# A quarter of layer B's input projection in seven block products instead of eight

## The chip, the cores and the metric

The kernel runs on one core of a Trainium2 chip. The core has a matrix engine (TensorE, PE in the profile), a vector engine (VectorE, DVE), a scalar engine (ScalarE, ACT), a general engine (GpSimd, POOL) and a queue that issues the transfers (SyncE, SP). Each engine works through its own list of instructions in order, and semaphores between the engines tell when an operand is ready or a buffer is free. Matmuls read their operands from SBUF and write to PSUM, which has eight banks of 128 x 512 float32 values.

The metric is the device time of one execution in microseconds. "Before" is the median of three runs.

## The reference

The reference is a two-layer encoder trunk for 256 tokens of width 2048 in float32. Layer A uses latent attention with 16 heads, layer B differential attention with 8 heads. Both add their result to the residual. What matters here is layer B:

```
z = rms_norm(x, norm_g) @ w_in            # 2048 -> 8192
q, k, v, gate = split(z)                  # 2048 each, 8 heads of 256
q, k = rms_norm per half head (128), times gains
p = softmax(q1 k1 + bias) - lam * softmax(q2 k2 + bias)
o = rms_norm(p @ v, subln) * (1 - lam_init)
out = x + (o * silu(gate)) @ w_out        # 2048 -> 2048
```

The projection `x @ w_in` is 256 x 2048 times 2048 x 8192.

## The kernel before

**Precision by splitting.** [...] To come near float32, each operand is split into a high part (a cast) and a low part (the value less the high part), and each product is made of three matmuls, `mm3`: high x high, low x high, high x low (lines 122 to 125). The three appear in the profile as L123, L124 and L125.

**Weights.** The weights stream from memory in chunks of 256 rows (two contraction tiles of 128) by 512 columns. `stream` (line 105) loads a chunk into one of four `raw` buffers (SP), ACT casts it into `whi` (L118), and DVE subtracts to give `wlo` (L119). There are three `whi` and three `wlo` buffers, so splits run at most some two chunks ahead of PE. `project` (line 127) then does 12 matmuls of width 512 a chunk: two contraction tiles, two token tiles of 128, three parts.

**Tokens.** The activations stand feature-major: `x1h` and `x1l` hold, for each of 16 contraction tiles, 128 features by 256 tokens. They are the stationary operand, the weights move.

**Layer B by heads.** For head h, block 2h of the weights gives q and k (512 columns), accumulated in the two PSUM banks of pool `psg` (named pg), and block 2h+1 gives v and the gate, in pool `psu` (pu). Each block is 8 chunks. Around them stand, per head:

- `qk_b`: squares of q and k by ACT (junk), a sum on DVE (ssb), a reciprocal root on POOL (fb), a multiplication on DVE (qk)
- `qk_t`: transposes of qk by PE (ptb), split by ACT and DVE into bh and bl
- `soft_b`: scores (psb), softmax and difference (eb) on DVE and ACT
- `p_b`: transposes of eb (ptpb), split into phb and plb
- `vg_b`: v split into vhb and vlb, the gate (sgb)
- `av_b`: the product with v (pob, 12 matmuls of width 256), then the sub-norm: ACT squares (junk), DVE (sso), POOL's root (fo), DVE (fo), and the gated result gob
- `go_b`: transposes of gob (pto), split into goh2 and gol2 for the output projection

The functions are called in an order that puts several chunks of the projections between one step and the next (lines 744 to 758), so that PE has matmuls to do while the other engines work through a chain. The final order on each engine is set when the program is scheduled: instructions that are ready in the scheduler's own reckoning can move ahead of others on their engine.

Between the layers, `add_a` adds layer A's output to the residual, and `x1_t(n)` transposes a quarter of it (ptx) and splits it into x1h and x1l. The last, `x1_t(3)`, follows the first two chunks of head 0's q and k.

## Time and profile before

| quantity | value |
|---|---|
| runs | 847.14, 847.34, 848.98 us; median 847.34 |
| span of the profiled execution (first to last instruction) | 845.0 us |
| median of the runs less that span | 2.3 us |
| busy PE, DVE, ACT, POOL in the span | 835.9, 564.6, 488.0, 86.4 us |
| one head of layer B (from ptb to ptb) | 48.29 us |
| granted TensorE clock, mean | 1.000 |

Rows of the timeline start with the start time and the length, both in us from the span's start; then come the engine, the line, the operation, and what is written from what; "x2" means that several instructions were merged into one row, whose length runs from the first's start to the last's end. In square brackets stands how long the engine was idle before, and what it waited for. A matmul's length counts its way through the array, so matmuls in a row overlap: their starts give the pace. Rows of the windows give a stretch, its length, busy time and number of instructions of PE, PE's weight loads, DVE, ACT and POOL, then the granted clock, the busy share of the DMA engines and GB/s. Grouped rows give the total busy time, the mean in ns, and the idle time before.

### The profile page before, as it was taken

How to read it: one execution, taken by the hardware profiler on the slowest of the kernel's cores; microseconds unless marked ns; L12 is line 12 of the kernel's file. 1: busy time of each engine (PE TensorE's matmuls, PEld its weight loads, DVE VectorE, ACT ScalarE, POOL GpSimd, SP SyncE). 2: the span in 40 equal slices, each digit the busy share in tenths (PEclk: the TensorE clock that was granted, in tenths of full speed). 3: DMA queues.
4: the chain of work that ended last, by engine and by line, in shares of the span. 5: the costliest groups of instructions: out<-in, count | busy, mean ns of one | idle time of the engine just before them, and what ended most of it. 6: DMA issues, size and time to landing. Idle time of an engine off the chain costs nothing.

```text
span 845.0 us, 11706 instructions
## 1 busy us (share of the span) xinstructions
PE 835.9 (99%) x4187; PEld 714.5 (85%) x4187; DVE 564.6 (67%) x968; ACT 488.0 (58%) x995; POOL 86.4 (10%) x113
## 2 busy tenths in 40 slices
PE   8999999999999999999999999999999999999998
PEld 6988888889888888888888888888888888888886
DVE  6968678788787866555647565565756566565543
ACT  7656687677767656555555465555555564554331
POOL 2300221122202200000010010010001000000000
PEclk9999999999999999999999999999999999999999
DMA  8755544534444645555555555554555555455661
GB/s 268 256 197 162 166 147 146 176 116 162 144 144 149 248 154 180 180 186 177 185 175 174 175 175 175 175 175 150 193 181 175 175 175 171 168 184 198 219 211 70
DMA packets 42954, 148.59 MB, mean 176 GB/s; under 512 B 5008, under 2 KB 6032, under 8 KB 42640
## 3 DMA queue, kind: packets, MB, share of 16 engines
q1 hardware_dynamic: 42896, 147.84, 52.5%
q8 instruction: 33, 0.54, 0.3%
q14 instruction: 25, 0.20, 0.1%
HBM read 145.73 MB, written 2.10 MB: 175 GB/s over the span
## 4 chain that ended last, share of the span: by engine, by line
PE 94%; DVE 3%; DMA 1%; ACT 1%; issue 0%; SPq 0%; POOL 0%; DVEq 0%; ACTq 0%
PE pu L123 14%; PE pu L125 14%; PE pu L124 14%; PE pg L124 13%; PE pg L123 13%; PE pg L125 13%; DVE wlo L119 1%; PE ptb L651 1%; PE ptn L430 1%; PE ptp L484 1%; PE pa L124 1%; DMA raw<-in_wz 1%; PE pa L125 1%; PE pa L123 1%; DVE xl L152 1%; PE ps L462 0%
## 5 line engine op out<-in xcount | busy, mean ns | idle before, releaser
L119 DVE TENSOR_TENSOR wlo<-raw,whi 128x1024 fp32r<-128x1024 f32 (+4 forms) x278 | 328.6, 1191 | 189.8 <-ACT whi L118 189.5
L118 ACT CAST whi<-raw 128x1024 fp32r<-128x1024 f32 (+3 forms) x277 | 282.2, 1025 | 233.6 <-PE pg L125 102.6
L123 PE MATMUL pu<-whi,x1h 128*128 128x512 f32 x256 | 101.3, 396 | 0.0
L123 PE MATMUL pg<-whi,x1h 128*128 128x512 f32 x256 | 100.5, 392 | 0.0
L125 PE MATMUL pu<-whi,x1l 128*128 128x512 f32 x256 | 99.9, 390 | 0.0
L124 PE MATMUL pu<-wlo,x1h 128*128 128x512 f32 x256 | 99.8, 390 | 0.0
L124 PE MATMUL pg<-wlo,x1h 128*128 128x512 f32 x256 | 99.7, 390 | 0.0
L125 PE MATMUL pg<-whi,x1l 128*128 128x512 f32 x256 | 99.7, 389 | 0.0
L125 PEld LDWEIGHTS pu<-whi,x1l 128*128 128x128 f32 x256 | 48.1, 188 | 10.2
L125 PEld LDWEIGHTS pg<-whi,x1l 128*128 128x128 f32 x256 | 48.1, 188 | 10.1
L123 PEld LDWEIGHTS pg<-whi,x1h 128*128 128x128 f32 x256 | 48.1, 188 | 9.5
L124 PEld LDWEIGHTS pg<-wlo,x1h 128*128 128x128 f32 x256 | 48.1, 188 | 9.4
L124 PEld LDWEIGHTS pu<-wlo,x1h 128*128 128x128 f32 x256 | 48.2, 188 | 9.2
L123 PEld LDWEIGHTS pu<-whi,x1h 128*128 128x128 f32 x256 | 48.1, 188 | 9.2
L123 PE MATMUL pg<-whi,xh 128*128 128x512 f32 (+1 forms) x128 | 49.8, 391 | 1.9 <-ACT whi L118 1.3
L124 PE MATMUL pg<-wlo,xh 128*128 128x512 f32 (+1 forms) x128 | 48.7, 381 | 1.9 <-DVE wlo L119 1.9
L123 PE MATMUL pg<-whi,goh 128*128 128x512 f32 x128 | 50.5, 395 | 0.0
L123 PE MATMUL pu<-whi,goh 128*128 128x512 f32 x128 | 50.1, 392 | 0.0
L124 PE MATMUL pg<-wlo,goh 128*128 128x512 f32 x128 | 49.9, 390 | 0.0
L125 PE MATMUL pg<-whi,gol 128*128 128x512 f32 x128 | 49.9, 390 | 0.0
L124 PE MATMUL pu<-wlo,goh 128*128 128x512 f32 x128 | 49.9, 390 | 0.0
L125 PE MATMUL pu<-whi,gol 128*128 128x512 f32 x128 | 49.9, 389 | 0.0
(246 smaller groups left out, 1551.1 us busy)
## 6 DMA issues: line engine op xcount, KB each, us to landing
raw<-in_wB SPq DMA_DIRECT2D x128, 512.0 KB, 3.2
raw<-in_wgA SPq DMA_DIRECT2D x32, 512.0 KB, 3.5
raw<-in_woA SPq DMA_DIRECT2D x32, 512.0 KB, 3.3
raw<-in_woB SPq DMA_DIRECT2D x32, 512.0 KB, 3.2
raw<-in_wkvu SPq DMA_DIRECT2D x16, 512.0 KB, 4.3
raw<-in_wz SPq DMA_DIRECT2D x15, 544.0 KB, 5.7
raw<-in_wqu SPq DMA_DIRECT2D x16, 384.0 KB, 3.1
x<-in_x SPq DMA_DIRECT2D x1, 2048.0 KB, 10.0
```

Source lines behind the costliest of these rows:

```text
L118: (V.tensor_copy if after_first and a == 0 else A.copy)(hi[:, a:b], raw[:, a:b])
L119: V.tensor_tensor(lo[:, a:b], raw[:, a:b], f32(hi[:, a:b]), ALU.subtract)
L123: T.matmul(o, shi, mhi, start=start, stop=False)
L124: T.matmul(o, shi, mlo, start=False, stop=False)
L125: T.matmul(o, slo, mhi, start=False, stop=stop)
L152: V.scalar_tensor_tensor(lo, src, g, f32(hi), ALU.mult, ALU.subtract)
L430: T.transpose(pt[:, h, t * P:(t + 1) * P], src[:, t, h, :NOPE], ident)
L484: T.transpose(pt[:, c, t * P:(t + 1) * P], e[:, t, c * P:(c + 1) * P], ident)
L651: T.transpose(pt[:, m, t * P:(t + 1) * P], qk[:, t, 2 * i + m, :], ident)
```

## The change

The first two of the eight chunks of each block (`FAST = 2`, a quarter of the contraction) are no longer multiplied straight. They are taken as a 2 x 2 by 2 x 2 block product: rows are the two token tiles, the inner index is the first or second contraction tile of a chunk, columns are the head's two weight blocks (q and k, v and gate). Straight that is eight block products, each summed over the two chunks. The change forms seven, by a known scheme:

- On the token side four sums of x tiles, made once after `x1_t(0)` by `sums`: ACT scales, POOL adds and subtracts, ACT and DVE split them into `sh` and `sl`.
- On the weight side four differences per head, t1, t2, t3 and t4, by DVE from the row blocks b11, b12, b21 and b22. `rows` loads a row block with one transfer (the same contraction tile of both chunks, 512 columns each). b22 is loaded twice.
- `form` splits a difference or a row block in the buffers whi and wlo (named fhi and flo), and `product` does 6 matmuls of width 512 with it, for two chunks and three parts.
- Four products (`shared`, steps 0 to 3) go to a PSUM bank of the pool `patt` (named pa), and ACT and DVE join them in SBUF in the tiles d0 to d3. The other three start the accumulation of the remaining six chunks in pg (two of them) and pu (one).
- `qk_b` and `vg_b` first add the accumulated banks into d0 and d2, or d1 and d3, and go on from these SBUF tiles where they read PSUM before.

The `shared` steps of head h+1 are called between the chunks of v and gate of head h; for head 0 all of them come in a row after layer A, with the first two products of its q and k, ahead of `x1_t(3)`. To make room in SBUF, buffers that only layer A uses go into a pool `la` that is closed ahead of layer B's pool `lb`.

Two places show how the order moves. The first is PE at head 2's `av_b` and `go_b`, where buffer numbers tell the tiles apart (fhi_5419 and flo_5420 hold the split of t4, whi_5430 the next chunk). Before, the transposes and their neighbours:

```order
L124 MATMUL pg_5211<-wlo_5311,x1h_3548 128x512
L125 MATMUL pg_5211<-whi_5310,x1l_3549 128x512
L733 MATMUL pto_5327<-ident_81,gob_5270 128x128 x4
L123 MATMUL pg_5210<-whi_5337,x1h_3548 128x512
L124 MATMUL pg_5210<-wlo_5338,x1h_3548 128x512
```

In the change:

```order
L128 MATMUL pob_5447<-vlb_5380,phb_5350 128x256
L129 MATMUL pob_5447<-vhb_5379,plb_5351 128x256
L839 MATMUL pto_5526<-ident_84,gob_5469 128x128 x2
L127 MATMUL pg_5404<-fhi_5419,x1h_3557 128x512
L839 MATMUL pto_5526<-ident_84,gob_5469 128x128 x2
L127 MATMUL pg_5403<-whi_5430,x1h_3557 128x512
L128 MATMUL pg_5404<-flo_5420,x1h_3557 128x512
```

Before, three chunks (36 matmuls) of the next head's q and k stood between pob and pto; now the transposes of gob follow pob's last matmul directly, and the product with t4 comes behind the first two of them. The second place is DVE at the same point of the program. Before, from the gate to gob:

```order
L669 SCALAR_TENSOR_TENSOR sgb_5201<-sgb_5201,pu_4991 128x256
L119 TENSOR_TENSOR wlo_5293<-raw_5291,whi_5292 128x1024
L119 TENSOR_TENSOR wlo_5311<-raw_5309,whi_5310 128x1024
L719 TENSOR_SCALAR sso_5261<-sso_5261 128x2
L722 TENSOR_TENSOR fo_5267<-fo_5267,r1h_4020 128x2
L725 SCALAR_TENSOR_TENSOR gob_5270<-pob_5248,fo_5267,sgb_5201 128x256 x2
```

In the change, from the second join of vg_b (L766; the first stands just ahead) to the split of t4:

```order
L766 TENSOR_TENSOR d3_4790<-pu_5141,d3_4790 128x512
L156 SCALAR_TENSOR_TENSOR vlb_5380<-d1_4788,r1x_4100,vhb_5379 128x256
L775 SCALAR_TENSOR_TENSOR sgb_5381<-sgb_5381,d1_4788 128x256
L676 TENSOR_TENSOR d1_5239<-pa_5390,d1_5239 128x512
L156 SCALAR_TENSOR_TENSOR vlb_5380<-d3_4790,r1x_4100,vhb_5379 128x256
L775 SCALAR_TENSOR_TENSOR sgb_5381<-sgb_5381,d3_4790 128x256
L677 TENSOR_TENSOR d3_5241<-pa_5390,d2_5240 128x512
L690 TENSOR_TENSOR t1_5417<-rows_5405,t2_5233 128x1024
L825 TENSOR_SCALAR sso_5460<-sso_5460 128x2
L828 TENSOR_TENSOR fo_5466<-fo_5466,r1h_4102 128x2
L831 SCALAR_TENSOR_TENSOR gob_5469<-pob_5447,fo_5466,sgb_5381 128x256 x2
L160 TENSOR_TENSOR flo_5420<-t1_5417,fhi_5419 128x1024
```

Joins and the difference t4 (in t1's buffer) now stand between the gate and the sub-norm, and the split of t4 behind gob.

The core of the diff, with renamed buffers of layer A left out:

```diff
+FAST = 2
...
+    only_a.close()
+    lb = ctx.enter_context(tc.tile_pool(name="lb", bufs=1))
...
+    def sums(c, pt):
+        xf = lb.tile([P, 2, S], F32, tag="t1", name="xf", padded_shape=[P, 2, 512])
+        for j in range(2):
+            A.activation(xf[:, j, :], pt[:, j, :], AF.Copy, scale=gB_t[:, 2 * c + j:2 * c + j + 1])
+        x00, x01, x10, x11 = (xf[:, j, t * P:(t + 1) * P] for t in range(2) for j in range(2))
+        s = lb.tile([P, 4, P], F32, tag="t3", name="s", padded_shape=[P, 8, P])
+        G.tensor_tensor(s[:, 0], x10, x11, ALU.add)
+        G.tensor_tensor(s[:, 2], x00, x10, ALU.subtract)
+        G.tensor_tensor(s[:, 1], s[:, 0], x00, ALU.subtract)
+        G.tensor_tensor(s[:, 3], x01, s[:, 1], ALU.subtract)
+        split(sh[:, c], sl_[:, c], s)
...
+    def form(src):
+        hi = wp.tile([P, 1024], F32R, tag="whi", name="fhi", padded_shape=[P, WCH])
+        lo = wp.tile([P, 1024], F32R, tag="wlo", name="flo", padded_shape=[P, WCH])
+        split(hi, lo, src)
+        return hi, lo
...
+    def product(o, lhs, src, start, stop):
+        hi, lo = form(src)
+        for c in range(FAST):
+            sl = slice(c * 512, (c + 1) * 512)
+            mm3(o, *lhs(c), hi[:, sl], lo[:, sl], start and c == 0, stop and c == FAST - 1)
...
+    def shared(h, i):
+        if i == 0:
+            b11, b12, b22 = rows(2 * h, 0), rows(2 * h + 1, 0), rows(2 * h + 1, 1)
+            t1, t2, t3 = t_tile("t1"), t_tile("t2"), t_tile("t3")
+            V.tensor_tensor(t1, b12, b11, ALU.subtract)
+            V.tensor_tensor(t3, b22, b12, ALU.subtract)
+            V.tensor_tensor(t2, b22, t1, ALU.subtract)
+            state["t", h] = (b11, t2, t3, t1)
+            state["d", h] = [lb.tile([P, 512], F32, tag=f"d{j}", name=f"d{j}", bufs=1 + j % 2) for j in range(4)]
+        d11, d12, d21, d22 = state["d", h]
+        p = bank(patt)
+        product(p, (own(0, 0), summed(1), summed(2), summed(0))[i], state["t", h][i], True, True)
+        if i == 0:
+            A.copy(d11, p)
+        elif i == 1:
+            V.tensor_tensor(d12, p, d11, ALU.add)
+        elif i == 2:
+            V.tensor_tensor(d21, p, d12, ALU.add)
+        else:
+            V.tensor_tensor(d12, p, d12, ALU.add)
+            V.tensor_tensor(d22, p, d21, ALU.add)
...
+    def qk_mm(h, n):
+        if n == 0:
+            state["qa", h] = pair(psg)
+        acc = state["qa", h]
+        if n < 2:
+            b21 = state["b21", h] = rows(2 * h, 1) if n == 0 else state["b21", h]
+            if n == 0:
+                product(acc[0], own(0, 1), b21, True, False)
+            else:
+                t4 = t_tile("t1")
+                V.tensor_tensor(t4, b21, state["t", h][1], ALU.subtract)
+                product(acc[1], own(1, 1), t4, True, False)
+        else:
+            rest(acc, 2 * h, n - 2 + FAST, False)
+
+    def vg_mm(h, n):
+        if n == 0:
+            state["va", h] = pair(psu)
+            product(state["va", h][0], summed(3), rows(2 * h + 1, 1), True, False)
+        else:
+            rest(state["va", h], 2 * h + 1, n - 1 + FAST, n == 1)
...
-    mm_b(0, psg, 0, 2)
+    for i in range(4):
+        shared(0, i)
+    for n in range(2):
+        qk_mm(0, n)
     x1_t(3)
...
+    def qk_b(h):
+        d = state["d", h][0::2]
+        for t, acc in enumerate(state.pop(("qa", h))):
+            V.tensor_tensor(d[t], acc, d[t], ALU.add)
...
+    def vg_b(h):
+        d = state.pop(("d", h))[1::2]
+        for t, acc in enumerate(state.pop(("va", h))):
+            V.tensor_tensor(d[t], acc, d[t], ALU.add)
...
+    NQ, NV = 2 + KC - FAST, 1 + KC - FAST
...
     for h in range(BH):
-        vg_b(h, 0, 3)
+        last = h + 1 == BH
+        vg_steps(h, 0, 3)
         qk_t(h)
-        vg_b(h, 3, 5)
+        vg_steps(h, 3, 4)
+        if not last:
+            shared(h + 1, 0)
+        vg_steps(h, 4, 5)
         soft_b(h)
-        vg_b(h, 5, 7)
+        if not last:
+            shared(h + 1, 1)
+        vg_steps(h, 5, 6)
+        if not last:
+            shared(h + 1, 2)
         p_b(h)
-        vg_b(h, 7, KC)
...
+        vg_steps(h, 6, NV)
...
+            shared(h + 1, 3)
+            qk_steps(h + 1, 0, 3)
+            av_b(h)
+            qk_steps(h + 1, 3, 6)
+            go_b(h)
+            qk_steps(h + 1, 6, NQ)
```

## The prediction

> **What bounds the kernel now.** I read the page's busy times first, then its chain of work that ended last, then the windows over the heads of layer B.

> ```profile
> PE 835.9 (99%) x4187; PEld 714.5 (85%) x4187; DVE 564.6 (67%) x968; ACT 488.0 (58%) x995; POOL 86.4 (10%) x113
> ...
> PE 94%; DVE 3%; DMA 1%; ACT 1%; issue 0%; SPq 0%; POOL 0%; DVEq 0%; ACTq 0%
> ```

> TensorE is the bound and fills 94% of the chain. One head of layer B, between one ptb transpose and the next, in the windows (length, then busy time of each engine):

> ```profile
> 445.97:494.26 48.29, 48.29 (x234) 40.54 (x233) 29.87 (x48) 26.54 (x53) 3.79 (x3) 1.00 0.52 175
> ```

> PE never idles in 48.29 us; VectorE has 18.4 us spare, ScalarE 21.8. So taking matmuls away pays in full, as long as those two keep far enough ahead of PE. The price of a matmul comes from the first and last of 35 consecutive ones in the timeline (start, length):

> ```profile
> 429.70 0.39 PE L124 MATMUL pg<-wlo,x1h 128*128 128x512 f32 x1
> ...
> 437.42 0.39 PE L125 MATMUL pg<-whi,x1l 128*128 128x512 f32 x1
> ```

> 34 steps in 7.72 us: 0.227 us each, so a weight chunk of 12 matmuls holds PE for 2.72 us and a product of 6 for 1.36. The vector prices, back to back, are two chunk subtractions and two 512-wide adds of PSUM into SBUF; beside them one ScalarE cast:

> ```profile
> 492.67 2.35 DVE L119 TENSOR_TENSOR wlo<-raw,whi 128x1024 fp32r<-128x1024 f32 x2
> 366.41 1.28 DVE L568 TENSOR_TENSOR x<-pu,x 128x512 f32<-128x512 f32 x2
> 491.57 1.05 ACT L118 CAST whi<-raw 128x1024 fp32r<-128x1024 f32 x1 [1.19 <-PE pu L125]
> ```

> A single subtraction lasts 1.22,

> ```profile
> L119 DVE TENSOR_TENSOR wlo<-raw,whi 128x1024 fp32r<-128x1024 f32 x240 | 292.0, 1224 | 177.6 <-ACT whi L118 177.6
> ```

> so in the pair the first makes way after 1.13; a 512-wide add costs 0.64.

> **What is removed.** The two fast chunks cost 48 matmuls a head and will cost 7 x 2 x 3 = 42. Over 8 heads 48 matmuls go: 48 x 0.227 = **10.9 us** less PE work, and a head's own PE work falls to 48.29 - 1.36 = 46.93.

> **What is added off PE.** Per head three more splits and four weight differences (t1 to t4), 7 x 1.13 = 7.9 us of DVE, and eight 512-wide joins, 8 x 0.64 = 5.1: DVE goes from 29.87 to about 42.9 of 46.93. ACT gets three casts and a copy, some 3.8 us, and stands near 30. Both fit as totals, so the sum by totals alone costs them at nothing. But DVE keeps only 4 us of slack, and its work comes in bunches where PE has only 1.36 us per split. Loads become 17 instead of 16 of 512 KB a head; DMA was 0.52 busy in the window above, and all raw buffers come round a chunk or more before they are needed, so I price them at nothing and keep a late load as a rival.

> **What is moved: the transposes of go.** This is the largest term. Before, 36 matmuls stood between the last pob matmul and the pto transposes, from 469.12 to 477.31 below. In the changed order the pto transposes stand directly behind pob, in heads 0 to 6. What lies between the two is the chain of the sub-norm:

> ```profile
> 469.00 0.28 PE L125 MATMUL pob<-vhb,plb 128*128 128x256 f32 x1
> 469.12 0.40 PE L123 MATMUL pg<-whi,x1h 128*128 128x512 f32 x1
> 469.32 0.39 ACT L718 ACTIVATE junk<-pob 128x256 f32<-128x256 f32 x1 [0.34 <-PE pob L125]
> 470.34 0.17 DVE L719 TENSOR_SCALAR sso<-sso 128x2 f32<-128x2 f32 x1
> 470.59 0.69 POOL L92 TENSOR_TENSOR fo<-sso,nhalf 128x2 f32<-128x2 f32 x1 [14.42 <-DVE sso L719]
> 471.32 0.16 DVE L722 TENSOR_TENSOR fo<-fo,r1h 128x2 f32<-128x2 f32 x1 [0.81 <-POOL fo L92]
> 471.51 0.88 DVE L725 SCALAR_TENSOR_TENSOR gob<-pob,fo,sgb 128x256 f32<-128x256 f32 x2
> ...
> 477.31 0.60 PE L733 MATMUL pto<-ident,gob 128*128 128x128 f32 x4
> ```

> PE is free of pob at 469.12, and the first gob tile is there at 471.51 + 0.44 = 471.95. With a tenth for the signal PE must wait 2.9 us at pto. Two waits stand beside it:
> - Ahead of pob. The value tiles vhb and vlb now need the joins of d1 and d3 first. After pu's last matmul DVE has about 0.5 of a split left, then two joins 1.28, vlb 0.40, sgb 0.36, a third join 0.64 and the second vlb 0.40, together 3.6. PE has two products (2.72) and the three pob matmuls (0.36) that need only the first tile. It waits about 0.6.
> - Behind pto. The split of t4 stands after gob on DVE and takes 1.13 from the end of the second gob (0.44 after the first); PE has the four transposes and two matmuls meanwhile, about 0.9. It waits about 0.7.

> The vlb and sgb steps are these rows:

> ```profile
> 462.96 0.48 DVE L152 SCALAR_TENSOR_TENSOR vlb<-pu,r1x,vhb 128x256 fp32r<-128x256 f32 x1 [0.20 <-ACT vhb L151]
> 463.36 0.41 DVE L669 SCALAR_TENSOR_TENSOR sgb<-sgb,pu 128x256 f32<-128x256 f32 x1
> ```

> Sum 0.6 + 2.9 + 0.7 = 4.2 us a head, seven times: **+29.4**. Behind the waiting transposes on PE stand t4's product and all chunks of the next q and k; nothing else there can run. Bounds: 0, 2.8 and 0.3 if DVE comes early (3.1 a head; no wait can be below nothing, and the chain has nothing left to drop); 1.5, 3.5 and 1.5 if it comes a split late (6.5). I take the middle, from the rows.

> **The ptb transposes, all heads.** From pg's end to q and k normalised took

> ```profile
> 485.45 0.28 ACT L637 ACTIVATE junk<-pg 128x128 f32<-128x128 f32 x1 [0.95 <-PE pg L125]
> ...
> 485.93 0.39 PE L123 MATMUL pu<-whi,x1h 128*128 128x512 f32 x1
> ...
> 491.46 1.29 DVE L641 TENSOR_TENSOR qk<-pg,fb 128x512 f32<-128x512 f32 x2 [1.75 <-POOL fb L92]
> ...
> 494.10 1.03 PE L651 MATMUL ptb<-ident,qk 128*128 128x128 f32 x8
> ```

> PE left pg at 485.93, so the first qk tile was ready 6.2 later (491.46 + 0.64) and PE came at 8.2. Now a join stands first (+0.7), ACT casts one chunk ahead of the squares and one more among them (+0.85, +1.05), and a split stands ahead of the second ssb (+0.4): ready at 9.2, while PE comes after a product, two chunks and seven matmuls, 1.36 + 5.44 + 1.59 = 8.39. That is a wait of 0.8 in seven heads, 0.4 in the last, which has no next head to prepare: **+6.0**; bounds 0 and 12.

> **The start.** Six products follow out_a(3) in a row. From its end until the first whole chunk's low half is there, DVE does two adds (1.28), four splits and t4 (5 x 1.13), four joins (2.56), four x1l (2 x 0.87), small ones (0.7) and that low half (1.13), in all 13.1, with about 0.8 of waiting for casts: 13.9. PE then has 11 matmuls left (2.5) and is through at 16.4, where its own work is 6 x 1.36 + 0.87 (the ptx transposes) + 2.72 = 11.75. **+4.6**; bounds 2.5 and 6.5.

> ```profile
> 374.57 0.87 DVE L152 SCALAR_TENSOR_TENSOR x1l<-ptx,gains_t,x1h 128x256 fp32r<-128x256 f32 x2
> ...
> 372.31 0.87 PE ptx L576 x8
> ```

> **The token sums.** Two chains of four 128x128 operations on POOL, priced by

> ```profile
> L413 POOL TENSOR_TENSOR rt<-qn,ropc 128x128 f32<-128x128 f32 x16 | 11.6, 728 | 52.2 <-ACT qn L403 52.2
> ```

> at 2.9 us each. ACT waits for them in its queue, ahead of two weight casts whose cover was 2.72 us: **+1.5**, bounds 0 and 3.

> **Sum.** -10.9 + 29.4 + 6.0 + 4.6 + 1.5 = +30.6. The profiled execution's span is 845.0 and the median of the runs 847.34, so 2.3 lies around it: 875.6 + 2.3 = **878 us**. The bounds together: -10.9 + 21.7 + 0 + 2.5 + 0 = +13 (861), and -10.9 + 45.5 + 12 + 6.5 + 3 = +56 (903), which needs every term at its worst.

> **Rivals.**
> 1. Short waits. Only what the order forces is paid: 3.35 a head at pto, 0.2 at ptb, 3 at the start: -10.9 + 23.5 + 1.6 + 3 = +17, **864.5**. For it: DVE has slack elsewhere and idled on casts in every chunk of the trace. Against: these places are where its added work is bunched. 0.16.
> 2. The clock drops in the new waits. At the trace's end PE is idle after 840.87 + 0.24:

> ```profile
> 840.87 0.24 PE pu L125
> 844.40:844.70 0.30, 0.00 (x0) 0.00 (x0) 0.00 (x0) 0.00 (x0) 0.00 (x0) 0.85 0.00 0
> 844.70:845.00 0.30, 0.00 (x0) 0.00 (x0) 0.00 (x0) 0.00 (x0) 0.00 (x0) 0.50 0.00 0
> ```

> The granted clock (the number before the last two) goes from 1.00 to 0.50 some 3.5 us after the last matmul. My wait is 2.9 with hardly a microsecond of work in the 1.6 after it. If it trips the gate, each head runs some 3.4 us at half speed and loses 1.7: 7 x 1.7 = 12 more, **890**. 0.14. [...]
> 3. A load is late. Four raw buffers now hold up to three row blocks at once, in pieces half as long. If a load lands in twice the page's 3.2 us in the bunch of each head, 2.5 more per head: 7 x 2.5 = 17, **895**. 0.05.

> ```profile
> raw<-in_wB SPq DMA_DIRECT2D x128, 512.0 KB, 3.2
> ```

> 4. Not slower: the wait at pto is covered. If PE's waits per head come below (10.9 - 4.6 - 1.5) / 7 = 0.7 us, the saving decides; with none the time is 847.3 - 10.9 + 6.1 = **842.5**. It needs the sub-norm chain in a quarter of the 2.9 us that its rows show, or other matmuls between pob and pto, and the order has none. 0.03. That the matmuls are not taken away is no rival: the changed order has 1,488 of them in this projection for 1,536.

> **How the numbers follow.** The first forecast has 0.62 (its own range 866 to 889). Rivals 1 to 4 have 0.16, 0.14, 0.05 and 0.03. Eight in ten lie between the short waits, opened a little below, and the dropped clock: 862 to 892. A measurement tells 0.2%, 1.7 us, from no change. Faster: rival 4 less a part, 0.02; same 0.01; slower 0.97.

> **What would show it.** In the changed trace: PE idle of 2.5 to 3.5 us before pto with gob as its releaser, seven times; idle before pob put to vlb, and before t4's product to its split; PE about 836 - 11 busy; DVE about 43 us in a head of 51 to 53; ptb waiting for qk by under 1.5; some 4 us of PE idle after out_a(3); granted clock 1.00 throughout. It is wrong if PE shows no gap between pob and pto, or if the largest idle is put to DMA.

## The result, and the profile after

The changed kernel takes 896.11 us (891.53 to 899.48) where the kernel before takes 847.59 beside it: a ratio of 1.0569, 95% interval 1.0541 to 1.0596. It is slower, as forecast, but by 48.5 us and not by 31, and it lies outside the range of 862 to 892.

The page of the changed kernel, busy times and the shares of its chain:

```profile
PE 852.6 (95%) x4139; PEld 719.3 (80%) x4139; DVE 664.4 (74%) x1090; ACT 517.6 (58%) x1033; POOL 98.2 (11%) x121
...
PE 80%; DVE 7%; ACT 5%; POOL 3%; issue 2%; DMA 2%; SPq 0%; DVEq 0%; ACTq 0%
```

TensorE has 48 matmuls fewer and is busy 16.7 us longer (835.9 before). So its instructions ran longer. The view by core gives the span and the mean granted clock:

```profile
core 0: 897.7 us, clock 0.976
```

It was 1.000 before: 2.4% of 897.7, some 21 us, is lost to half clock. What TensorE waited for in the changed kernel (us in total, times, longest):

```profile
PE pto L839 <- DVE gob L831: 19.6, 7, 2.8
PE ptb L756 <- DVE qk L746: 12.6, 8, 1.9
PE pg L128 <- DVE flo L160: 2.2, 5, 0.8
PE pg L127 <- ACT fhi L159: 1.9, 1, 1.9
```

The seven waits at pto, 2.8 us each with gob as their releaser, are the ones of the forecast. Windows of 2 us around the first of them (length, then busy time of PE, PEld, DVE, ACT and POOL with counts; the third number from the end is the granted clock):

```profile
429.00:431.00 2.00, 0.82 (x7) 0.62 (x6) 1.75 (x3) 1.11 (x5) 0.00 (x0) 1.00 0.00 0
431.00:433.00 2.00, 0.40 (x3) 0.41 (x3) 1.15 (x5) 2.00 (x3) 0.70 (x1) 0.71 0.65 186
433.00:435.00 2.00, 2.00 (x8) 1.66 (x7) 2.00 (x2) 1.14 (x2) 0.00 (x0) 0.50 0.19 76
435.00:437.00 2.00, 2.00 (x6) 1.52 (x6) 1.73 (x3) 0.26 (x1) 0.00 (x0) 0.50 0.39 102
437.00:439.00 2.00, 2.00 (x7) 1.56 (x6) 1.19 (x2) 1.16 (x2) 0.00 (x0) 0.58 0.80 291
439.00:441.00 2.00, 2.00 (x11) 1.61 (x10) 0.43 (x2) 0.70 (x1) 0.00 (x0) 1.00 0.59 205
```

Once PE is back at work it fits 6 to 8 matmuls into 2 us and not 11, until the clock returns. The same stands behind every pto in half-microsecond windows: the clock is at 0.50 for 3.41 us, sometimes for 6.83, and 1.7 or 3.4 us are lost. It stands behind the start too (377 to 384.5) and behind one ptb (681). Together these stretches lose 20.5 us; another 0.8 us lies behind the last matmul. In the stretch of layer B, changed kernel and then before:

```profile
360.00:842.00 482.00, 445.58 (x2006) 363.91 (x2005) 360.50 (x524) 258.55 (x480) 35.40 (x24) 0.96 0.52 167
```

```profile
360.00:842.00 482.00, 481.09 (x2279) 402.50 (x2277) 287.65 (x428) 248.86 (x464) 28.21 (x23) 1.00 0.53 176
```

PE's idle time went from 0.9 to 36.4 us. The spans differ by 52.7: 35.5 of idle time, 20.5 of half clock, less 10.9 of matmuls, and 7.6 that are recorded as busy. An estimate gives 4.5 of these: in each of the seven heads pob's fifth and sixth matmul together start 0.3 us late, and ahead of each of the fifteen waits at pto and ptb the last matmul counts some 0.16 us more than its pace, while it goes through the array (0.28 us for 0.12, or 0.39 for 0.227). The rest is open. DVE fills a head as forecast:

```profile
408.70:464.05 55.35, 50.77 (x227) 41.52 (x227) 42.13 (x63) 29.95 (x57) 4.76 (x3) 0.94 0.50 162
```

42.1 us of it (42.9 forecast), ACT 29.95 (30), while the head has grown to 53 to 57 us.

### The profile page after: what moved, and what is told of

It is laid out like the page before. It is cut to its first block, busy times and chain, and to the rows that moved or that the text cites. A ratio compares the mean times of both kernels' runs of the same rounds, so it can differ in the third digit from the quotient of the medians.

```text
span 897.7 us, 11799 instructions
## 1 busy us (share of the span) xinstructions
PE 852.6 (95%) x4139; PEld 719.3 (80%) x4139; DVE 664.4 (74%) x1090; ACT 517.6 (58%) x1033; POOL 98.2 (11%) x121
## 4 chain that ended last, share of the span: by engine, by line
PE 80%; DVE 7%; ACT 5%; POOL 3%; issue 2%; DMA 2%; SPq 0%; DVEq 0%; ACTq 0%
PE pg L128 12%; PE pg L129 12%; PE pg L127 12%; PE pu L129 9%; PE pu L128 9%; PE pu L127 9%; PE pa L128 2%; PE pa L129 2%; PE pa L127 2%; POOL fb L96 2%; DVE flo L160 2%; ACT whi L122 2%; ACT junk L742 1%; DVE wlo L123 1%; PE ptb L756 1%
## 5 line engine op out<-in xcount | busy, mean ns | idle before, releaser
L123 DVE TENSOR_TENSOR wlo<-raw,whi 128x1024 fp32r<-128x1024 f32 (+3 forms) x246 | 289.3, 1187 | 143.2 <-ACT whi L122 142.6
L122 ACT CAST whi<-raw 128x1024 fp32r<-128x1024 f32 (+4 forms) x245 | 247.7, 1021 | 193.1 <-PE pg L129 99.4
L129 PE MATMUL pg<-whi,x1l 128*128 128x512 f32 x192 | 77.5, 404 | 0.0
L127 PE MATMUL pu<-whi,x1h 128*128 128x512 f32 x192 | 76.7, 400 | 0.0
L128 PE MATMUL pu<-wlo,x1h 128*128 128x512 f32 x192 | 76.1, 396 | 0.0
L129 PE MATMUL pu<-whi,x1l 128*128 128x512 f32 x192 | 75.3, 392 | 0.0
L129 PE MATMUL pg<-whi,xl 128*128 128x512 f32 (+1 forms) x128 | 48.7, 381 | 0.0
L159 ACT CAST fhi<-t 128x1024 fp32r<-128x1024 f32 x32 | 33.5, 1046 | 23.8 <-PE pu L129 20.4
L129 PE MATMUL pu<-whi,m 128*128 128x384 f32 (+1 forms) x128 | 46.4, 362 | 0.0
L127 PE MATMUL pu<-whi,m 128*128 128x384 f32 (+1 forms) x128 | 46.4, 362 | 0.0
L128 PE MATMUL pu<-wlo,m 128*128 128x384 f32 (+1 forms) x128 | 46.3, 362 | 0.0
## 6 DMA issues: line engine op xcount, KB each, us to landing
raw<-in_wB SPq DMA_DIRECT2D x96, 512.0 KB, 4.0
rows<-in_wB SPq DMA_DIRECT2D x40, 512.0 KB, 4.2
raw<-in_wgA SPq DMA_DIRECT2D x32, 512.0 KB, 3.4
raw<-in_woA SPq DMA_DIRECT2D x32, 512.0 KB, 3.5
raw<-in_woB SPq DMA_DIRECT2D x32, 512.0 KB, 3.2
raw<-in_wkvu SPq DMA_DIRECT2D x16, 512.0 KB, 4.1
```

What stands on the lines that cost most here:

```text
L122: (V.tensor_copy if after_first and a == 0 else A.copy)(hi[:, a:b], raw[:, a:b])
L123: V.tensor_tensor(lo[:, a:b], raw[:, a:b], f32(hi[:, a:b]), ALU.subtract)
L127: T.matmul(o, shi, mhi, start=start, stop=False)
L128: T.matmul(o, shi, mlo, start=False, stop=False)
L129: T.matmul(o, slo, mhi, start=False, stop=stop)
L159: A.copy(hi, src)
```

## The experiments

Two theories were at hand. **The clock**: the waits come out nearly as forecast, and a wait of 2.8 us is enough to halve the clock behind it. **VectorE's load**: 42 us of vector work in a head stall TensorE wherever they stand, and the low clock only follows from that. A third reading, waits alone with a clock that drops for another reason, was kept beside them.

**1. The moved transposes alone, in the kernel before.** All eight block products; only TensorE's order is forced.

```diff
-        av_b(h)
-        nxt(2, 5)
-        go_b(h)
-        nxt(5, KC if h + 1 < BH else 7)
+        if h + 1 < BH:
+            with tc.issue_after(state["mm"].ins):
+                av_b(h)
+            go_b(h)
+            with tc.issue_after(state["pto"].ins):
+                nxt(2, KC)
...
```

`state["mm"]` is the last matmul of the two chunks ahead, `state["pto"]` the last transpose.

> The kernel before, with all eight block products, in which only the order on TensorE is forced: in heads 0 to 6 the four pto transposes stand directly behind the twelve pob matmuls and all further chunks of the next head's q and k behind pto. Nothing else is changed. Theory of the clock: a wait of 2.8 us at pto is enough to halve the granted clock behind it, so each head pays 2.8 and some 2.2 of half clock: 847.5 + 7 x 5.0 = 882 us (875 to 890), with a granted clock of 0.50 within 3 us behind every pto. Theory of the waits alone (the low clock of the changed kernel has another cause, such as its products of six matmuls): 847.5 + 7 x 2.8 = 867 us (864 to 870), granted clock 1.00. Theory of VectorE's load (the wait is long because VectorE has 42 us of work in a head): with VectorE at 30 us a head the wait is under 2 us and the time under 862.

Measured: 880.14 us, ratio 1.0389 (1.0373 to 1.0404). What TensorE waited for at pto:

```profile
PE pto L733 <- DVE gob L725: 19.6, 7, 2.8
```

Four windows around the second pto, with columns as above:

```profile
474.00:476.00 2.00, 0.50 (x5) 0.29 (x3) 1.40 (x2) 1.15 (x5) 0.20 (x1) 1.00 0.61 225
476.00:478.00 2.00, 0.73 (x4) 0.63 (x5) 1.04 (x3) 0.00 (x0) 0.50 (x1) 0.61 0.75 242
478.00:480.00 2.00, 2.00 (x7) 1.61 (x6) 0.52 (x2) 0.95 (x2) 0.00 (x0) 0.50 0.06 25
480.00:482.00 2.00, 2.00 (x6) 1.55 (x5) 0.44 (x1) 0.00 (x0) 0.00 (x0) 0.50 0.00 0
```

VectorE is busy for 3.4 of these 8 us, and the wait is the same 2.8 us and the clock falls the same way: seven waits make 19.6 us, and the half clock in this trace loses 13.7. The theory of the clock said 882, the waits alone 867, VectorE's load under 862. So the place of these four transposes alone, with none of the seven-product change in it, costs 33 us, two thirds of the 48.

**2. Work in the wait.** The changed kernel with 24 matmuls more in each of heads 0 to 6.

```diff
+        if h + 1 < BH:
+            hot = patt.tile([P, NT, BV], F32, tag="pa", name="hot")
+            for _ in range(2):
+                for t in range(NT):
+                    tq = slice(t * P, (t + 1) * P)
+                    for c in range(2):
+                        mm3(hot[:, t, :], ph[:, c, tq], pl[:, c, tq], vh[:, c, :], vl[:, c, :], c == 0, c == 1)
```

> The changed kernel with 24 matmuls more in each of heads 0 to 6: the pob products twice over into a bank that nobody reads, between pob and pto, so that TensorE has some 2.9 us of work where it waits 2.8. The outputs stay those of the reference. Theory of the clock: the low clock that now costs some 15 of 20.5 us behind pto goes, and the time falls although work is added: 896 - 15 + 7 x 0.5 = 884 us (880 to 889). Theory of the waits alone: nothing is gained and a little lost, 896 + 7 x 0.6 = 900 us (897 to 903).

Measured: 884.18 us, ratio 1.0441 (1.0425 to 1.0456): 11.9 us less than the changed kernel, with 168 matmuls added. Its span and clock, and what TensorE waited for:

```profile
core 0: 882.6 us, clock 0.998
```

```profile
PE ptb L756 <- DVE qk L746: 10.7, 8, 1.8
...
PE pto L846 <- DVE gob L838: 1.7, 7, 0.2
```

The chain that pto waits for is no shorter here (the first gob is written 2.7 to 2.8 us after pob's end in both kernels, and pto starts 4.9 to 5.0 us after pob's first matmul, for 4.6 to 4.7); only the idle time is filled. That the time falls all the same shows that the low clock behind pto cost at least these 11.9 us.

**3. t4's product late.** Three whole chunks can run between pob and pto.

```diff
-            qk_mm(h, n)
+            qk_mm(h, (0, 2, 3, 4, 1, 5, 6, 7)[n] if h > 0 else n)
```

> The changed kernel, in which for heads 1 to 7 the product with t4 is taken behind three whole chunks of q and k and not ahead of them, so that those chunks can run between pob and pto; t4 itself is still formed early. Same matmuls, same VectorE work. Theory of the pto wait with the clock: what stands between pob and the next v and g now costs 39 us more than its matmuls; without the wait 896 - 39 = 857 us (853 to 863), no idle time put to gob, no low clock behind pob. Theory of the waits alone: 896 - 20 = 876 us (873 to 879). Theory of VectorE's load: the stall comes back at the next place where TensorE needs a split, and the time stays over 885.

Measured: 867.56 us, ratio 1.0246 (1.0225 to 1.0266): 28.5 us less, where the clock said 39 and the waits alone 20. What TensorE waits for now:

```profile
PE ptb L762 <- DVE qk L752: 14.3, 8, 1.9
PE pg L128 <- DVE wlo L123: 7.8, 10, 1.2
```

No wait at pto is left, and the mean granted clock is 0.997, with one drop. But a new wait stands behind pob, 0.8 us in each head: the low half of the next chunk, whose subtraction is queued on VectorE behind the joins and the v and g steps. This is the part of the load theory that holds: a stall taken away comes back smaller at the next place.

**4. GpSimd's power beside a subtraction, in the kernel before.** In the changed kernel the power for fb takes 2.5 us where it took 1.64, and a subtraction runs with it. Head 1 of the changed kernel:

```profile
460.46 1.22 DVE L662 TENSOR_TENSOR t<-rows 128x1024 f32<-128x1024 f32 x1
...
460.63 2.54 POOL L96 TENSOR_TENSOR fb<-ssb,nhalf 128x8 f32<-128x8 f32 x1 [28.80 <-DVE ssb L743]
```

```diff
+        with tc.issue_after(last.ins):
+            V.tensor_tensor(scr, x1[:, 0, :1024], x1[:, 1, :1024], ALU.subtract)
```

> The kernel before with one more VectorE instruction in each head of layer B: a 128x1024 subtraction of two SBUF operands into a scratch tile, placed directly behind the second ssb, so that it runs while GpSimd takes the power for fb. Nothing reads its result. If VectorE's subtraction slows GpSimd, fb lasts about 2.5 us for 1.64 before in heads 0 to 7; if the 2.5 us of the changed kernel come from elsewhere it stays at 1.6 to 1.7. The time stays within 1 us of before in either case, since TensorE reached ptb 2.0 us after qk was ready.

Measured: 847.43 us. fb in the groups by line of the kernel before, and of this one:

```profile
L92 POOL TENSOR_TENSOR fb<-ssb,nhalf 128x8 f32<-128x8 f32 x8 | 13.1, 1641 | 152.5 <-DVE ssb L638 152.5
```

```profile
L92 POOL TENSOR_TENSOR fb<-ssb,nhalf 128x8 f32<-128x8 f32 x8 | 20.3, 2538 | 152.5 <-DVE ssb L638 152.5
```

A subtraction of 1.22 us lengthens a power of 1.64 us by 0.9 in all eight heads. In this run the next weight subtraction follows at once and also runs beside the power (in head 2 it starts at 491.27, and the power lasts from 490.31 to 492.86); in head 1 of the changed kernel, above, the one subtraction is alone and the power lasts as long. The runs give the 0.9 us; by what it comes about they do not show.

**5. q and k's steps later.**

```diff
-        vg_steps(h, 0, 3)
-        qk_t(h)
-        vg_steps(h, 3, 4)
+        vg_steps(h, 0, 4)
         if not last:
             shared(h + 1, 0)
+        qk_t(h)
...
```

> The changed kernel with the steps of q and k moved later in each head: the ptb transposes stand behind four pieces of v and g and the first product of the next head instead of inside the third chunk, the score matmuls and ptpb move back with them. Same matmuls, same VectorE work; pto stays where it is. Theory that the ptb wait is the chain of joins, squares and power and that TensorE comes too early for it: the 12.6 us of idle time at ptb and the 2 us of half clock behind it go, 896 - 14 = 882 us (878 to 888), if pob does not now wait for its own operand. Theory of VectorE's load: the chain itself is late because VectorE is full there; later transposes leave it as late, and the time stays over 892.

Measured: 889.87 us, ratio 1.0515 (1.0489 to 1.0540), 6 us less than the changed kernel, for 14 expected: a miss for both numbers. Waits:

```profile
PE pto L839 <- DVE gob L831: 19.6, 7, 2.8
PE pu L128 <- DVE wlo L123: 5.4, 7, 1.0
PE pg L128 <- DVE flo L160: 3.1, 7, 0.8
...
PE pob L127 <- ACT phb L159: 1.8, 7, 0.3
```

ptb is gone from the list. In its place stand 1.0 us before the low half of the chunk behind ptb, which VectorE takes after qk and t2, and 0.3 at pob. Of 12.6 us, about 5 were won. The trace also lost less to half clock, 12.0 us for the 20.5 of the changed kernel's; so the 6 us between the medians can't be put to the waits alone. That the ptb wait was partly the chain that came late and partly VectorE's bunch around it is a reading of the waits that are left, and not shown apart.

**6. Head 0's products mixed with layer A's last block.**

```diff
-    out_a(3, psu, 2, KC)
-    add_a(3)
...
-    for i in range(4):
-        shared(0, i)
-    for n in range(2):
-        qk_mm(0, n)
+    for c in range(2, KC):
+        out_a(3, psu, c, c + 1)
+        if c < 6:
+            shared(0, c - 2)
+        else:
+            qk_mm(0, c - 6)
+    add_a(3)
+    qk_mm(0, 2)
```

> The changed kernel in which the six products of head 0 stand between the chunks 2 to 7 of layer A's last output block instead of behind them in a row; everything from head 0's whole chunks on is as in the changed kernel. Theory that the start costs its waits and the half clock behind them because splits are bunched there: 6.4 us go, 896 - 6.4 = 889.7 us (887 to 892), and the granted clock stays 1.00 until head 0's pto. Theory that the splits and joins of head 0 take VectorE's time wherever they stand: under 3 us are gained, over 893.

Measured: 893.59 us, ratio 1.0545 (1.0527 to 1.0564). In the trace head 0's v and g begin at 392.60 and not at 398.42, 5.8 us sooner, the clock stays at 1.00 until the first pto, and the span is 892.0 for 897.7. The medians differ by 2.5 only. How much half clock follows the waits differs from one execution to the next (mean granted clock 0.976 to 0.984 over the four of the changed kernel), and the times of the changed kernel spread over 8 us where those before spread over 2; so the trace speaks for the start as a place of 6 us, while the median is the number of the second theory (over 893). The two are not settled here.

**7. The three moves together**, with nothing else.

> The changed kernel with the three moves together: t4's product behind three chunks (867.6 us alone), q and k's steps later, head 0's products mixed with layer A's last block. If the three places are independent: 867.6 - 14 - 6.4 = 847 us (843 to 853), with some 8 us of idle time left at the first chunk behind pob, whose low half comes late. Theory of VectorE's load: a stall that is taken away at one place comes back at the next, over 856 us.

Measured: 855.76 us, ratio 1.0106 (1.0086 to 1.0126), 9 above the 847 that was forecast and between the two theories' ranges. That forecast took 14 and 6.4 us for two of the moves; with what the single runs measured (28.5, 6.2 and 2.5 us) the sum would be 858.8, so the three together gain 3 us more than apart. The granted clock is 1.00 throughout, and all that is left in layer B, but for 0.4 us at ptb, is

```profile
PE pg L128 <- DVE wlo L123: 7.7, 9, 1.2
PE pu L128 <- DVE wlo L123: 6.8, 7, 1.1
```

the chunk behind pob and the chunk behind ptb. Both wait for a split that stands behind bunched VectorE work.

**8. The same with VectorE's bunches spread.**

```diff
-            shared(h + 1, 3)
-            qk_steps(h + 1, 0, 3)
+            qk_steps(h + 1, 0, 1)
+            p_b(h)
+            qk_steps(h + 1, 1, 2)
+            vg_b(h)
+            qk_steps(h + 1, 2, 3)
             av_b(h)
+            shared(h + 1, 3)
...
```

`vg_b` holds the joins of v and g, vlb and sgb, and is taken out of `vg_steps`.

> The three moves, and VectorE's work at the turn of a head spread as well: the joins of v and g and what follows from them stand behind the split of the next head's second piece, the fourth shared product and its two joins behind pob, and t4 is formed behind them. Same matmuls, same number of VectorE instructions. If only the bunches cost time: the 8 us at the first chunk behind pob go too, 847 - 7 = 840 us (836 to 846), which is the saving of 48 matmuls (10.9 us) less some waits of a few tenths a head, and faster than before. Theory of VectorE's load (42 of some 48 us a head are too much to be laid out without stalls): over 847 us.

Measured: **845.04 us, ratio 0.9975 (0.9965 to 0.9984)**: faster than the kernel before, by 2.4 us or 0.25% (the interval stays below 1, though single executions of the two overlap), and 51 us faster than the changed kernel with the same arithmetic. Two of its heads:

```profile
441.04:488.58 47.54, 47.48 (x227) 39.38 (x226) 41.94 (x63) 29.96 (x57) 3.80 (x3) 1.00 0.58 188
...
583.68:632.14 48.46, 47.49 (x227) 39.38 (x226) 41.84 (x63) 29.95 (x57) 4.70 (x3) 1.00 0.58 184
```

VectorE has the same 42 us of work and now fits beside 47.5 us of TensorE: its load as such was not the cause. A head falls from 48.29 to 47.54 in the better case, 0.75 for the 1.36 of the six matmuls; 0.5 of PE's 47.48 us is more than its matmuls account for (46.93), and what they are is open. In three heads a wait of 0.93 to 0.97 before the chunk behind ptb is left, in a fourth 0.2, and POOL's 4.70 for 3.80 is the power at 2.55 us again. So of the 10.9 us of matmuls taken away only 2.4 arrive.

**9. t2 one step later in that kernel**, behind the low half that TensorE waits for.

> The three moves spread out (845.0 us) and t2 formed one step later, behind the low half of the next v and g chunk, for which TensorE waited 0.8 to 1.0 us in four heads. If that wait is only t2's subtraction ahead of it: 845.0 - 3 = 842 us (840 to 844). If VectorE is full there, the wait comes back at the product with t2 and the time stays at 844 to 847.

Measured: 845.94 us, ratio 0.9984 (0.9972 to 0.9996). The wait that it was to remove had stood in three heads (0.93 to 0.97 us) and, at 0.2, in a fourth; the expectation counted four of 0.8 to 1.0. In its place stands

```profile
PE pa L128 <- DVE flo L160: 1.5, 4, 0.5
```

up to 0.5 us at a product that waits for its split. The time is the same within its spread (843.5 to 849.8). That is the load theory's number.

**10. The power kept free of the subtraction, in the changed kernel.**

```diff
-            V.tensor_tensor(t3, b22, b12, ALU.subtract)
-            V.tensor_tensor(t2, b22, t1, ALU.subtract)
+            with (tc.issue_after(state["lastqk"].ins) if h else ExitStack()):
+                V.tensor_tensor(t2, b22, t1, ALU.subtract)
...
```

`lastqk` is the second qk; t3's subtraction is held behind it in the same way, in the next step.

> The changed kernel in which, for heads 1 to 7 of the seven products, the subtractions of t2 and t3 are held on VectorE until the second qk is written, so that none of them runs while GpSimd takes the power for fb. Same work; the ptb transposes stand two rows earlier on TensorE. Theory that fb is slow because of the subtraction beside it: fb falls from 2.55 to 1.6 us, q and k are ready 0.9 earlier in heads 0 to 6, and the time falls by about 7 x 0.9 = 6 us, 890 (886 to 893). Theory that the ptb wait is set by the joins and squares ahead of the power: no change beyond 2 us, 894 to 898.

Measured: 897.54 us, ratio 1.0600 (1.0585 to 1.0616), no gain. fb and ptb in its head 1:

```profile
457.21 1.64 POOL L96 TENSOR_TENSOR fb<-ssb,nhalf 128x8 f32<-128x8 f32 x1 [27.94 <-DVE ssb L747]
...
459.72 0.41 PE L760 MATMUL ptb<-ident,qk 128*128 128x128 f32 x2 [1.76 <-DVE qk L750]
```

The power is back at 1.64 and qk comes 0.9 sooner, but ptb waits as long as it did. The order had put the transposes four matmuls earlier, 4 x 0.227 = 0.9 us, so TensorE also came 0.9 sooner. What the slower power costs in time is therefore not shown by this run; by the chain it is 0.9 of the 1.75 at ptb.

**11. Waits of graded length**, in the kernel of experiment 1, with 2 to 18 matmuls in the wait.

```diff
+            with tc.issue_after(state["mm"].ins):
+                for i in range((2, 6, 8, 10, 12, 14, 18)[h]):
+                    T.matmul(hot[:, 0, :], ph[:, 0, :P], vh[:, 0, :], start=True, stop=True)
```

> The kernel before with pto forced behind pob as in the run above, and with 2, 6, 8, 10, 12, 14 and 18 matmuls of 128x256 (0.12 us each, into a bank that nobody reads) behind pob in heads 0 to 6, so that the wait at pto is graded: 2.6, 2.1, 1.85, 1.6, 1.35, 1.1 and 0.65 us. If a fixed length of the wait decides on the clock, a granted clock of 0.50 shows behind the longer waits and behind no shorter one, with the edge between 1.2 and 2.6. If the gate looks at windows that run freely, waits of 1.6 to 2.1 drop it in some heads and not in others, in no order of length. Time: 847.5 + 7 x 2.9 = 867.5 and 1.7 us for each drop, 869 to 877.

> As the graded kernel before, with the seven lengths dealt out otherwise over heads 0 to 6: 12, 4, 10, 2, 14, 8 and 6 matmuls, so waits of 1.35, 2.3, 1.6, 2.6, 1.1, 1.85 and 2.1 us. If a fixed length decides, the same lengths drop the clock as in the other; if free windows decide, 1.6 to 2.1 come out differently here and there. Time 869 to 877.

Measured: 872.17 and 872.20 us. Two heads of the first and two of the second, with the wait in brackets:

```profile
423.63 1.11 PE L738 MATMUL pto<-ident,gob 128*128 128x128 f32 x4 [2.54 <-DVE gob L730]
476.40 0.83 PE L738 MATMUL pto<-ident,gob 128*128 128x128 f32 x4 [2.06 <-DVE gob L730]
```

```profile
684.14 0.83 PE L738 MATMUL pto<-ident,gob 128*128 128x128 f32 x4 [1.87 <-DVE gob L730]
735.62 0.83 PE L738 MATMUL pto<-ident,gob 128*128 128x128 f32 x4 [2.11 <-DVE gob L730]
```

The clock fell behind 2.54 and 2.06 in the first, behind 2.29 and 2.59 in the second, and behind nothing else; 2.11 and 1.87 left it at 1.00. So lengths are not in order at the edge: 2.06 fell and 2.11 did not.

That is what the second reading, windows that run freely, expects. Within a trace all beginnings and ends of the half clock lie whole multiples of 3.413 us apart: in the changed kernel a stretch of it lasts 3.413 or 6.827 us, and its nine beginnings from 377.24 on lie 16, 17, 16, 15, 16, 9, 7 and 17 times 3.413 us apart. The stretches of 3.413 us counted from such a beginning, forward and back, are called clock windows here. Cut into them, the rows around the wait of 2.06 (first kernel), around that of 2.11 (second kernel), and around the only wait of 2.8 at a pto that left the clock at 1.00 (2.83, in the kernel of experiment 5) are

```profile
474.64:478.05 3.41, 1.65 (x9) 1.28 (x10) 1.48 (x5) 0.48 (x2) 0.69 (x1) 1.00 0.45 154
478.05:481.47 3.42, 3.42 (x10) 2.64 (x9) 0.70 (x2) 0.48 (x1) 0.00 (x0) 0.50 0.00 0
```

```profile
731.30:734.71 3.41, 2.21 (x19) 2.01 (x17) 1.39 (x2) 2.00 (x5) 0.56 (x1) 1.00 0.46 172
734.71:738.12 3.41, 2.50 (x12) 1.99 (x13) 1.62 (x5) 0.95 (x2) 0.14 (x1) 1.00 0.43 159
738.12:741.54 3.42, 3.42 (x17) 2.83 (x16) 1.61 (x2) 1.05 (x1) 0.00 (x0) 1.00 0.00 0
```

```profile
642.03:645.44 3.41, 1.83 (x12) 1.28 (x11) 2.81 (x5) 1.45 (x5) 0.21 (x1) 1.00 0.00 0
645.44:648.85 3.41, 1.76 (x9) 1.33 (x10) 2.86 (x5) 2.70 (x4) 0.48 (x1) 1.00 0.48 154
648.85:652.27 3.42, 3.42 (x17) 2.83 (x16) 3.42 (x5) 1.60 (x3) 0.00 (x0) 1.00 0.55 174
```

The length of a row less PE's busy time is the idle time in it. The wait of 2.06 leaves 1.76 us idle in one clock window, and the next has half clock. The border between two clock windows cuts the wait of 2.11 into 1.20 and 0.91, and that of 2.83 into 1.58 and 1.65, and nothing follows. Over the 14 traces of this case, from 20 us on, all 50 clock windows at full clock with at least 1.83 us idle were followed by half clock, 4 of 12 with 1.72 to 1.82, and none of more than 3300 with 1.68 or less. So the idle time in a clock window, with an edge between 1.68 and 1.83 us, tells apart in these traces which waits half clock follows; the length of a wait, 2.06 against 2.11 or 2.83, does not.

## Why the prediction was wrong

- **What bounds the kernel: right.** TensorE is the bound; idle time on it was paid in full.
- **VectorE's and ScalarE's totals: right** (42.1 and 29.95 us), and costing them at nothing as totals was right too in the main: in the eighth run the same totals cost 3.1 us of waits.
- **The pto transposes: the wait was right, what follows it was wrong.** Forecast 2.9 us a head behind pob, measured 2.8 in all seven. Ahead of pob 0.6 was forecast and 0.3 came: from pob's first matmul to pto it takes 4.69 us, of which 1.43 are the matmuls and 2.93 lie behind the last one's pace, 2.8 of them recorded as idle. The 0.7 behind pto were about 0.2. The term came out as some 24 us for 29.4, before the clock.
- **The clock: this is the step that failed.** The sum left the clock at 1.00 through a wait of 2.9 us. The second rival had the clock falling in the new waits and was given 0.14, because the end of the trace showed the clock falling only 3.5 us after the last matmul, and 2.9 is less. But those 3.5 us were a single case, and the clock at the end of a program was read as a threshold. The fall there came at 844.61 (0.85 is the mean of 844.40 to 844.70), so a clock window of 3.41 us (experiment 11) began at 841.19, by chance 0.08 us after the last matmul's end at 841.11, and the fall came at its end. In the seven heads the clock fell 2.0 to 4.8 us after pob's end, in four of them when PE was already back at work, at the end of a clock window with 1.76 to 2.55 us of idle time. Waits alone give 897.7 - 20.5 = 877.2 for the forecast span of 875.6; the miss is the size of the clock loss. That the other terms come so near to their sum is in part luck, since a ptb term that was too small makes up for pto, start and sums that were too large. Experiments 1 and 2 show the clock loss from both sides. The rival's 3.4 us at half speed stood in no view of before; the runs show 3.41 in 39 of 44 cases and 6.83 in five. Its price, 12 us for seven drops, was too small as well: two of the seven lasted twice as long, and the start and one ptb added 5.
- **The ptb transposes: mis-sized.** Forecast 6.0, measured 12.6 of idle time in eight heads. q and k were ready 10.2 us after PE left pg for 9.2 forecast. 0.9 of that is GpSimd's power beside the subtraction, which the forecast priced at its old 1.64. In the last head, where 0.4 was forecast and 1.75 came, the power took 1.64; there PE came to ptb after 33 matmuls and not 37, 0.8 us sooner than forecast, and the chain took 0.5 longer.
- **The start: 4.6 forecast, 6.4 measured**, of which 3.4 are half clock; the waits alone, about 3, were below the term.
- **The token sums: 1.5 forecast, nothing came**; PE had no idle time between 300 and 367 us. The late load (third rival) didn't come either: no wait of PE is put to a DMA.
- **That the order and not the arithmetic decides** was in the forecast only as its fourth rival, as a wait covered by other matmuls. The eighth run is near that case, at 845.0 us for its 842.5.

Against the profiled span the miss is 897.7 - 875.6 = 22.1 us: the clock with 20.5, ptb with 6.6 more, pto (-5.4), start (-1.6) and sums (-1.5) with 8.5 less, and 3.5 that the views don't give apart.

## What to carry to other kernels

In these traces half clock followed 37 of 38 waits of 2.29 to 2.83 us on TensorE and cost 1.7 or 3.4 us each time; a new wait of that length is to be priced with it, once for each place where it recurs. What told the cases apart was the idle time within one clock window of 3.41 us, so a wait near 2 us cost or did not cost by where it fell (7 of 11 between 1.88 and 2.11 us). That short waits close together add up is not shown. When matmuls are replaced by vector work, lay out what VectorE has to do between two points where TensorE needs it, and keep whole chunks of independent matmuls for the long chains; a total that fits says little: the same 42 us of VectorE a head went with 896.11 and with 845.04 us. Before pricing a small GpSimd instruction in a chain from an old trace, look at what VectorE will be doing beside it (1.64 or 2.54 us here).
